# An encoder block on one core: the output projection by seven block products, the memory halves split early, the mixer's residual by accumulating DMAs, the last stores on ScalarE's queue

## The chip, the cores and the metric

The kernel runs on one core of a Trainium2 chip. The metric is the device time of one execution in microseconds (us). Beside the times of plain runs there is one profiled execution, whose trace holds every instruction of the engines and every DMA. The engines are PE (TensorE, with PEld for its weight loads), DVE (VectorE), ACT (ScalarE), POOL (GpSimd) and SP (SyncE, which here only issues DMAs). A "Q" behind an engine's name stands for its sequencer.

## The reference

One layer of an encoder on `x` (512 tokens x 2048, float32), with three sub-layers on the residual stream:

```
h   = rms_norm(x, g_mix_pre);  proj = h @ w_in
mix = concat(diff_attention(8 heads), stick_breaking(8 heads)) @ w_out   # each head normalised on its own
x   = x + rms_norm(mix, g_mix_post)
h   = rms_norm(x, g_mem_pre);  k, v = split(rms_norm(mem, g_mem_kv) @ w_mkv)   # 256 memory tokens, 4 heads
x   = x + rms_norm(softmax(h @ w_mq @ k^T / sqrt(512)) @ v @ w_mo, g_mem_post)
h   = rms_norm(x, g_ffn_pre);  gu = h @ w_gate_up
x   = x + rms_norm((silu(gu[:5632]) * gu[5632:]) @ w_down, g_ffn_post)
```

All inputs and the output are float32.

## The kernel before

Matrix products run on PE in the type fp32r. To keep float32 accuracy each operand is split into a high half h (a rounding copy, on ACT) and a low half l (the difference, on DVE), and each product is made of three matmuls, h·h, h·l and l·h. So each pass over a tile of 128x512 results costs three matmuls.

Weights come in chunks of 128x1024 (512 KB). `Weights` holds the list `chunks` in the order of use; a chunk is loaded into one of the `raws` tiles (five, NR; eight, NW, in some stages) on SP's queue (L120), split by ACT (L131) and DVE (L132) into one of three slots of `parts`, and used by PE (L254). A raw tile is free again once its chunk is split. A chunk's split runs up to two chunks ahead of PE.

`w_v` (and the gate, up and down projections) use a seven-product block scheme, class `Blocks`: the 2x2 blocks of activations and weights are combined so that seven block products stand for eight. Sums of weight blocks are formed while loading: `"load"` with two blocks is a plain load and an accumulating DMA (POOL's queue, L122 and L140) into the same raw tile, `"add"` accumulates one more block onto a raw tile that an earlier product used. The sums of the activations' blocks (`in_forms`) and the sums of the seven results (`evict`) are DVE work.

The output projection `w_out` does not use it: 4 column blocks x 4 token tiles x 16 k tiles x 3 matmuls of 128x512 = 768 matmuls, its 40 chunks (the last column block is done in two halves and loaded twice) by plain loads. The mixed heads come from `subnorm`, one 128x512 tile `mixT` per head, split by `split_mix` into `big`. `Sub.evict` multiplies each result by the post gain; `Sub.residual` (L1157) adds the residual `xres`, which `load_x` (L1103) has loaded, and stores the sum to `x2_d` (L1159); `turn` transposes the result on PE (L1166) and splits it into `big`. `Sub.chain` runs these steps for one token tile, in small steps between PE's matmuls (`side`, `side2`).

The memory attention is folded into its weights: `fold_keys` multiplies `w_mq` by the memory keys (two pairs of heads, 16 rows r each, 24 matmuls of 128x256 each), then come scores and softmax, then `fold_values` on `w_mo`. Keys and values of the memory are made at the start and lie in DRAM (`kT_d`, `vT_d`) as float32; `load_keys` and `load_values` load them back (`kraw`, `vraw`) and split them just before use.

At the end, the eight results of token tiles 0 and 1 are finished by `finish_dma` (scaled, the residual added by an accumulating DMA of POOL's queue, L1135, stored by SP, L1136), the eight of tiles 2 and 3 by `finish` (DVE, L1142; stored by SP, L1145).

The order on every engine is set when the program is built: `fill` runs a step of the side generators every so many matmuls, and a scheduler places each instruction on its engine.

## Time and profile before

| | |
|---|---|
| median of 3 runs (lowest, highest) | 2673.8 us (2672.63, 2677.52) |
| the profiled execution: its own time | 2675.06 us |
| the profiled execution: span from first to last instruction | 2673.2 us |
| busy share of the span: PE, DVE, ACT, POOL | 99%, 62%, 50%, 10% |
| mean granted TensorE clock | 0.997 of full speed |
| DMA | 491.14 MB, mean 184 GB/s |

Line numbers (L254) are those of the kernel before. "a<-b" is an instruction that writes tile a from tile b; 128x512 is partitions x elements. In a row of waits the engine on the left waited for the instruction on the right. The lines of the changed kernel have other numbers: L254, L257 and L258 became L262, L265 and L266; L120, L131, L132 and L140 became L128, L139, L140 and L148; L1136 and L1145 became L1186 and L1195; L1166 became L1238.

### The profile page before, as it was taken

Reading aid. Unit: us, or ns where it says so; the run is one execution under the profiler, and the core shown is the slowest. Engines: PE = TensorE matmul, PEld = TensorE weight load, DVE = VectorE, ACT = ScalarE, POOL = GpSimd, SP = SyncE. Lnnn points to the kernel's source line nnn. Section 1 sums busy time; section 2 is a strip of 40 time slices with the busy share of each in tenths; the row PEclk is TensorE's granted clock in tenths of the full one; section 3 lists DMA queues with packets and bytes.
Section 4 is the critical chain, followed back from the end, with each engine's and each line's share of the span. In section 5 each row is a group of like instructions: output and inputs, shape, how many; then the busy total and the mean of one; then the engine's idle time right before and its main releaser. Section 6 shows DMA issues by size and latency. Waiting matters only on the chain.

```text
span 2673.2 us, 33720 instructions
## 1 busy us (share of the span) xinstructions
PE 2638.9 (99%) x12608; PEld 2194.4 (82%) x12608; DVE 1667.2 (62%) x2295; ACT 1341.0 (50%) x1962; POOL 269.0 (10%) x319
## 2 busy tenths in 40 slices
PE   8999999999999999999999999999999999999997
PEld 7888887778888889988888888888888888878775
DVE  6796556775555366543577665555556568786776
ACT  5555434555665355432455444444444456554554
POOL 0001200000000000000001211211111121102112
PEclk9999999999999999999999999999999999999998
DMA  8889932222222374323558999988888998788888
GB/s 291 284 263 263 231 125 95 85 89 87 71 71 75 126 261 165 115 91 115 162 185 197 250 243 221 196 201 205 204 206 197 210 227 244 195 269 213 214 198 209
DMA packets 171077, 491.14 MB, mean 184 GB/s; under 512 B 18976, under 2 KB 29624, under 8 KB 170912
## 3 DMA queue, kind: packets, MB, share of 16 engines
q1 hardware_dynamic: 129376, 346.47, 38.8%
q0 software_dynamic: 41536, 142.51, 29.0%
q8 instruction: 99, 1.62, 0.3%
q14 instruction: 66, 0.54, 0.1%
HBM read 447.99 MB, written 43.54 MB: 184 GB/s over the span
## 4 chain that ended last, share of the span: by engine, by line
PE 89%; issue 6%; DMA 2%; DVE 1%; POOL 1%; ACT 1%; POOLq 0%; DVEq 0%; SPq 0%; ACTq 0%
PE ps L254 87%; DMA raws<-in_w_dn_dram 1%; PE ps L1509 1%; DVE parts L132 1%; POOL y_d L1625 1%; PE ps L1166 1%; DMA xnat<-in_x_dram 0%; ACT parts L131 0%; PE ps L978 0%; POOL raws L140 0%; DMA kT_d<-memev 0%; POOL raw L140 0%; DMA small<-in_gains_dram 0%; PE ps L1302 0%; DVE raws L137 0%
## 5 line engine op out<-in xcount | busy, mean ns | idle before, releaser
L254 PE MATMUL ps<-parts,big 128*128 128x512 f32 x4608 | 1068.5, 390 | 6.1 <-DVE parts L132 2.8
L132 DVE TENSOR_TENSOR parts<-raws,parts 128x1024 fp32r<-128x1024 f32 x551 | 672.8, 1223 | 555.9 <-ACT parts L131 551.7
L254 PEld LDWEIGHTS ps<-parts,big 128*128 128x128 f32 x4608 | 862.6, 188 | 189.3 <-DVE parts L132 7.5
L131 ACT CAST parts<-raws 128x1024 fp32r<-128x1024 f32 x551 | 579.6, 1052 | 697.1 <-PE ps L254 625.8
L254 PE MATMUL ps<-parts,form 128*128 128x512 f32 x2376 | 550.2, 390 | 2.8 <-ACT parts L131 1.6
L254 PEld LDWEIGHTS ps<-parts,form 128*128 128x128 f32 x2376 | 444.5, 188 | 97.7 <-DVE parts L132 3.6
L254 PE MATMUL ps<-big,parts 128*128 128x512 f32 x1536 | 380.5, 395 | 0.0
L254 PEld LDWEIGHTS ps<-big,parts 128*128 128x128 f32 x1536 | 281.8, 188 | 62.2 <-issue 3.7
L132 DVE TENSOR_TENSOR parts<-raw,parts 128x1024 fp32r<-128x1024 f32 x178 | 217.2, 1222 | 154.2 <-ACT parts L131 153.9
L131 ACT CAST parts<-raw 128x1024 fp32r<-128x1024 f32 x178 | 187.5, 1053 | 194.6 <-PE ps L254 151.0
L254 PE MATMUL ps<-memhl,parts 128*128 128x512 f32 (+1 forms) x1024 | 185.1, 343 | 8.8 <-DVE memhl L265 7.2
L254 PEld LDWEIGHTS ps<-memhl,parts 128*128 128x128 f32 x1024 | 158.9, 191 | 33.6 <-DVE memhl L265 7.2
L140 POOL DMA_DIRECT2D raws<-in_w_gu_dram x108 | 93.3, 864 | 827.3 <-DVE parts L132 699.2
L254 PE MATMUL ps<-khl,parts 128*128 128x256 f32 x768 | 96.2, 285 | 0.0
L418 POOL TENSOR_TENSOR small<-small 128x1 f32<-128x1 f32 (+2 forms) x18 | 12.5, 700 | 824.7 <-DVE small L417 805.6
L254 PEld LDWEIGHTS ps<-khl,parts 128*128 128x128 f32 x768 | 93.3, 192 | 0.2
L254 PE MATMUL ps<-big,pTh 128*128 128x512 f32 x256 | 80.1, 392 | 0.0
L254 PE MATMUL ps<-gh,big 128*128 128x512 f32 x256 | 79.2, 389 | 0.0
L955 ACT ACTIVATE e<-e,small 128x512 f32<-128x512 f32 (+3 forms) x64 | 35.5, 555 | 62.1 <-DVE small L953 62.1
L140 POOL DMA_DIRECT2D raw<-in_w_gu_dram x60 | 51.8, 864 | 114.5 <-DVE parts L132 114.5
L254 PE MATMUL ps<-parts,inh 128*128 128x512 f32 x192 | 59.1, 389 | 0.0
L254 PEld LDWEIGHTS ps<-gh,big 128*128 128x128 f32 x256 | 48.1, 188 | 10.0
(791 smaller groups left out, 2361.9 us busy)
## 6 DMA issues: line engine op xcount, KB each, us to landing
raws<-in_w_gu_dram POOLq DMA_DIRECT2D x113, 512.0 KB, 6.4
raws<-in_w_gu_dram SPq DMA_DIRECT2D x80, 512.0 KB, 4.2
raws<-in_w_qk_dram SPq DMA_DIRECT2D x64, 512.0 KB, 3.4
raw<-in_w_gu_dram POOLq DMA_DIRECT2D x63, 512.0 KB, 5.9
raw<-in_w_gu_dram SPq DMA_DIRECT2D x60, 512.0 KB, 4.2
aq<-actT_d SPq DMA_DIRECT2D x90, 256.0 KB, 5.1
raws<-in_w_dn_dram SPq DMA_DIRECT2D x41, 512.0 KB, 4.9
raws<-in_w_out_dram SPq DMA_DIRECT2D x40, 512.0 KB, 3.4
```

The source lines that it names most:

```text
L131: self.nc.scalar.copy(h, r)
L132: self.nc.vector.tensor_tensor(l, r, h.bitcast(F32), op=ALU.subtract)
L140: self.nc.gpsimd.dma_start(r, self.chunks[m][3], accum_op=ALU.add)
L254: nc.tensor.matmul(o, l, r, start=start, stop=stop, skip_group_check=True)
L418: nc.gpsimd.tensor_tensor(dst, t, mhalf[:, 0:n], op=ALU.pow)
L955: nc.scalar.activation(es[m][:, 0:n], es[m][:, 0:n], AF.Exp, bias=nmx[:, m : m + 1], accum_out=z[:, m : m + 1],)
L1166: nc.tensor.transpose(tp[:, k * P : (k + 1) * P], h[:, k * P : (k + 1) * P], ident)
L1509: nc.tensor.transpose(tp[:, k * P : (k + 1) * P], f[:, k * P : (k + 1) * P], ident)
L1625: nc.gpsimd.dma_start(y_d[t, cb], c, accum_op=ALU.add)
```

## The change

1. `w_out` is computed by `Blocks` in seven products for each of two pairs of column blocks: 7 x 2 x (4 chunks x 2 k x 2 token halves x 3) = 672 matmuls. Products 1 and 7, which only need heads 0 to 7, run first for both pairs, between the last heads. 40 plain loads and 32 accumulating loads bring the weights; products 7 and 5 have both in one chunk. `mix_forms` makes the sums of activation blocks on DVE.
2. The residual after `w_out` is an accumulating DMA: `residual_dma` scales the result by r1 and the gain in one DVE instruction, POOL's queue adds `x` from DRAM, and SP stores the sum. `xres` is not loaded there any more.
3. `split_memory` splits keys and values during the heads' stage and stores both halves (`khl_d`, `vhl_d`); `load_keys` and `load_values` load halves and split nothing.
4. The stores of `finish` go to ScalarE's queue.
5. `subnorm` squares on ACT instead of DVE and ends in two instructions of 256 columns.

```diff
+EARLY, ORDER_MIX = (1, 7), (5, 3, 6, 2, 4)
+MAKE_MIX = {1: ("load", (0, 0)), 7: ("load", (1, 1), (0, 1)), 2: ("load", (1, 0)),
+            3: ("load", (1, 1)), 5: ("load", (0, 0), (0, 1)), 6: ("add", 5, (1, 1)),
+            4: ("add", 6, (1, 0))}
+MIX_WAIT = 8.0, 4.0, 22.0, 10.0
...
-    for cb in range(NCB):
-        wm("w_out", cb, range(8))
-    wm("w_out", NCB - 1, range(8))
+    for i in EARLY:
+        for cbs in col_pairs:
+            wf("w_out", cbs, 0, 4, (i,), MAKE_MIX)
+    for cbs in col_pairs:
+        wf("w_out", cbs, 0, 4, ORDER_MIX, MAKE_MIX)
...
+    def split_memory():
+        for src, dst in ((kT_d, khl_d), (vT_d, vhl_d)):
+            for k2 in range(KT // 2):
+                r = u2(F32, "mraw")
+                dma(r, src[2 * k2 : 2 * k2 + 2].rearrange("k p m -> p k m") if src is kT_d
+                    else src[k2])
+                yield 6.0
+                for k in range(2):
+                    o = u2(s="mhl")
+                    split(o[:, 0], o[:, 1], r[:, k])
+                    dma(dst[2 * k2 + k], o.bitcast(F32))
+                    yield 6.0
...
-            dma(self.dst[t * P : (t + 1) * P, cb * 512 : (cb + 1) * 512], y)
+            nc.scalar.dma_start(self.dst[t * P : (t + 1) * P, cb * 512 : (cb + 1) * 512], y)
...
+        def residual_dma(self, t):
+            s1, r1 = st(), st()
+            nc.vector.tensor_reduce(s1, self.ss[t], axis=AX.X, op=ALU.add)
+            pow_rstd(r1, s1, 1)
+            ss2 = st(4)
+            for cb in range(NCB):
+                y = self.y[t, cb]
+                nc.vector.scalar_tensor_tensor(
+                    y, y, r1, self.g[cb], op0=ALU.mult, op1=ALU.mult
+                )
+                nc.gpsimd.dma_start(
+                    y, self.src[t * P : (t + 1) * P, cb * 512 : (cb + 1) * 512], accum_op=ALU.add
+                )
+                yield 1.5
+            yield 8.0
+            for cb in range(NCB):
+                y = self.y[t, cb]
+                nc.scalar.activation(junk, y, AF.Square, accum_out=ss2[:, cb : cb + 1])
+                dma(self.dst[t * P : (t + 1) * P, cb * 512 : (cb + 1) * 512], y)
+            return ss2
...
     def load_keys(pair):
+        for k in range(8 * pair, 8 * pair + 8):
+            khl[k] = u2(s="khl")
+            dma(khl[k].bitcast(F32), khl_d[k])
+            yield 2
...
+    for i in EARLY:
+        for n, g in enumerate(pairs):
+            g.product(i)
+            done_mix.add((i, n))
+    mix_raw = wpool.tile([P, NW - NR, 1024], F32, name="mix_raw")
+    W.more([mix_raw[:, i] for i in range(NW - NR)], pairs[1].T[7, 1], n_mix)
+    for n, g in enumerate(pairs):
+        g.every = 1
+        for cb in g.cbs:
+            sub.load_g(cb)
+        for i in ORDER_MIX:
+            if n and i == 6:
+                side.add(load_keys(0))
+            g.product(i)
...
-    def load_values(c2s, early):
-        for c2 in c2s:
-            vr = u2(F32, "vraw")
-            dma(vr, vT_d[c2])
+    def load_values(cts, early):
+        for ct in cts:
+            if early:
+                vv = u2(s="vhl")
+                vhl[ct] = (vv[:, 0], vv[:, 1])
+            else:
+                vv = big[:, :, ct, 0:M]
+                vhl[ct] = (big[:, 0, ct, 0:M], big[:, 1, ct, 0:M])
+            dma(vv.bitcast(F32), vhl_d[ct])
```

Three places of the program's order show how it moves instructions. The first is SP's queue between the output projection and `fold_keys`, before the change: the stores `x_d` of the mixer's sums wait for DVE, and the first loads of `w_mq` stand behind all eight of tiles 0 and 1.

```order
L1159 DMA x_d<-y_7149 128x512 [waits DMAHW4_49,DVE_49]
L1159 DMA x_d<-y_7383 128x512 [waits DMAHW5_49,DVE_49]
L1159 DMA x_d<-y_7649 128x512 [waits DMAHW6_49,DVE_49]
L1159 DMA x_d<-y_7801 128x512 [waits DMAHW7_49,DVE_49]
L120 DMA raws<-in_w_mq_dram 128x1024 [waits DMAHW0_49,DVE_49]
L120 DMA raws<-in_w_mq_dram 128x1024 [waits DMAHW1_49,DVE_49]
```

The same place now; "DMASW" is a semaphore of POOL's queue, here that of the accumulating load of the same tile. The last row of `w_mq` ahead of the first store is the chunk of r = 4.

```order
L128 DMA raws<-in_w_mq_dram 128x1024 [waits DMAHW4_49,DMASW1_49,DVE_49]
L1231 DMA x_d<-p__932_7068 128x512 [waits DMAHW5_49,DMASW5_49]
L1231 DMA x_d<-p__982_7551 128x512 [waits DMAHW6_49,DMASW6_49]
L1231 DMA x_d<-p__952_7201 128x512 [waits DMAHW7_49,DMASW7_49]
L1231 DMA x_d<-p__1008_7927 128x512 [waits DMAHW0_49,DMASW0_49]
L128 DMA raws<-in_w_mq_dram 128x1024 [waits DMAHW1_49,DVE_49]
L1231 DMA x_d<-p__933_7070 128x512 [waits DMAHW2_49,DMASW1_49]
L128 DMA raws<-in_w_mq_dram 128x1024 [waits DMAHW3_49,DVE_49]
L1231 DMA x_d<-p__983_7553 128x512 [waits DMAHW4_49,DMASW2_49]
L128 DMA raws<-in_w_mq_dram 128x1024 [waits DMAHW5_49,DVE_49]
```

The stores now wait for accumulating DMAs, and the chunks of r = 5, 6 and 7 stand behind the fourth, the fifth and the sixth store. The second place is the start of `fold_values`: on ACT before the change, where the value halves are copied behind the last exponentials and one weight chunk,

```order
L1288 ACTIVATE ce_9682,small<-ps_9631,small 128x256 [waits DVE_49,PE_49]
L1288 ACTIVATE ce_9682,small<-ps_9631,small 128x256
L131 CAST parts<-raws 128x1024 [waits DMAHW3_49,PE_49]
L257 CAST big<-vraw_9688 128x256 [waits DMAHW1_49]
L257 CAST big<-vraw_9688 128x256
```

and on SP now, where the halves are loaded, each behind a wait for PE (the scores' last matmul that reads that place of `big`):

```order
L1429 DMA vhl_9666<-vhl_d 128x512 [waits PE_49]
L1429 DMA vhl_9692<-vhl_d 128x512 [waits PE_49]
L128 DMA raws<-in_w_mo_dram 128x1024 [waits DMAHW2_49,DVE_49]
L1429 DMA big<-vhl_d 128x2x256 [waits PE_49]
L1429 DMA big<-vhl_d 128x2x256 [waits DMAHW3_49,PE_49]
```

The copies left ACT and DVE, and 14 loads of 256 KB came to SP's queue. The third place is the end of the program. Before, SP has the last stores of tile 1 (L1136) and then the eight of tiles 2 and 3:

```order
L1136 DMA out_dram<-p__1756_19055 128x512 [waits DMAHW3_49,DMASW1_49]
L1136 DMA out_dram<-p__1770_19341 128x512 [waits DMAHW4_49,DMASW2_49]
L1136 DMA out_dram<-p__1779_19514 128x512 [waits DMAHW5_49,DMASW3_49]
L1145 DMA out_dram<-base_19176 128x512 [waits DMAHW6_49,DVE_49]
L1145 DMA out_dram<-p__1749_18982 128x512 [waits DMAHW7_49,DVE_49]
```

Now ACT has them, behind its last activation:

```order
L1728 ACTIVATE junk,small<-base_19695 128x512 [waits DVE_49,Activation_49]
L1195 DMA out_dram<-base_19351 128x512 [waits DMAHW6_49,DVE_49]
L1195 DMA out_dram<-p__1804_19157 128x512 [waits DMAHW7_49,DVE_49]
L1195 DMA out_dram<-p__1828_19569 128x512 [waits DMAHW0_49,DVE_49]
L1195 DMA out_dram<-y_19862 128x512 [waits DMAHW1_49,DVE_49]
L1195 DMA out_dram<-base_19353 128x512 [waits DMAHW2_49,DVE_49]
```

The semaphores DMAHW0 to DMAHW7 go round over all DMAs of SP and ACT. The eight stores of SP ahead of these use DMAHW6, 7, 0 to 5 in this order, so that the k-th store of ACT waits for the landing of SP's k-th store of L1186, as SP's own did before.

## Rows read from the trace of the kernel before

**Rows 1.** The page, its first and fourth parts: busy time of each engine with its share of the span, and the shares of the chain of work that ended last, by engine.

```profile
PE 2638.9 (99%) x12608; PEld 2194.4 (82%) x12608; DVE 1667.2 (62%) x2295; ACT 1341.0 (50%) x1962; POOL 269.0 (10%) x319
PE 89%; issue 6%; DMA 2%; DVE 1%; POOL 1%; ACT 1%; POOLq 0%; DVEq 0%; SPq 0%; ACTq 0%
```

**Rows 2.** Busy time of each engine by stretch of the span: the bounds in us, the length, then for each engine its busy time and number of instructions, the granted TensorE clock as a share of full speed, the busy share of the 16 DMA engines, GB/s. The stretches are the value projection `w_v`, the 16 heads and the output projection `w_out`.

```profile
187.00:340.00 153.00, 153.00 (x687) 126.89 (x686) 96.46 (x113) 73.38 (x86) 28.45 (x33) 1.00 0.98 249
340.00:823.00 483.00, 483.00 (x2376) 391.03 (x2375) 292.34 (x596) 264.19 (x483) 0.00 (x0) 1.00 0.27 87
823.00:994.00 171.00, 170.93 (x773) 141.65 (x772) 79.13 (x98) 71.24 (x114) 2.21 (x3) 1.00 0.47 155
```

**Rows 3.** All waits of PE in the span: what was waited for, us in total, times, longest.

```profile
PE ps L254 <- DVE memhl L265: 7.2, 1, 7.2
PE ps L254 <- DVE parts L132: 5.0, 11, 0.8
PE ps L254 <- ACT parts L131: 4.0, 6, 1.4
PE ps L254 <- ACT big L257: 1.4, 1, 1.4
```

**Rows 4.** The chain that ended last, in `w_out` (matmuls 128x512) and in `fold_keys` (128x256): start, us, engine, what, number of instructions.

```profile
873.42 105.93 PE ps L254 x466
...
1017.16 11.51 PE ps L254 x96
```

**Rows 5.** Two of the waits of all engines in the stretch of `w_v` from 187 to 340 us (us in total, times, longest); the answer has none of PE's matmuls, only PEld, the weight loads.

```profile
ACT parts L131 <- PE ps L254: 74.2, 49, 3.3
PEld ps L254 <- issue: 0.2, 1, 0.2
```

**Rows 6.** A stretch of 11 us in `w_v` and one of 20 us in the mixer's residual; columns as in rows 2.

```profile
231.00:242.00 11.00, 11.00 (x51) 9.09 (x50) 5.01 (x5) 5.37 (x7) 3.45 (x4) 1.00 1.06 211
...
1000.00:1020.00 20.00, 20.00 (x173) 20.00 (x172) 19.12 (x30) 19.63 (x41) 2.00 (x2) 1.00 0.82 295
```

**Rows 7.** The page's third part (DMA queue: packets, MB, time of their packets as a share of 16 engines' span), and DMA issues: tile and tensor, queue, number, KB each, median us from issue to landing.

```profile
q1 hardware_dynamic: 129376, 346.47, 38.8%
q0 software_dynamic: 41536, 142.51, 29.0%
...
raws<-in_w_v_dram POOLq DMA_DIRECT2D x20, 512.0 KB, 9.4
iraw<-in_w_v_dram SPq DMA_DIRECT2D x9, 512.0 KB, 7.1
raws<-in_w_mq_dram SPq DMA_DIRECT2D x32, 512.0 KB, 3.6
```

**Rows 8.** The accumulating loads of `w_v` by their line: the issue on POOL (ns min/median/max, first and last start) and the time from issue to landing.

```profile
L140 POOL DMA_DIRECT2D raws<-in_w_v_dram x20: 853/862/949, 192.7 to 312.5; - x20
...
DMA to landing us min/median/max: 5.2/9.4/11.4
```

**Rows 9.** Instructions of DVE and ACT by line and form: number, busy us, mean ns of one, idle before.

```profile
L132 DVE TENSOR_TENSOR parts<-raws,parts 128x1024 fp32r<-128x1024 f32 x551 | 672.8, 1223 | 555.9 <-ACT parts L131 551.7 <-DMA vr<-v_d 2.9 <-DMA xres<-in_x_dram 0.8
L258 DVE TENSOR_TENSOR big<-mixT,big 128x512 fp32r<-128x512 f32 x15 | 10.0, 687 | 1.3 <-ACT big L257 1.1
L131 ACT CAST parts<-raws 128x1024 fp32r<-128x1024 f32 x551 | 579.6, 1052 | 697.1 <-PE ps L254 625.8 <-issue 19.7 <-DMA raws<-in_w_dn_dram 18.1
```

**Rows 10.** The start of `fold_values` in order of time: PE, ACT and SP (start, us, what, number; in brackets the idle time before it and what ended that).

```profile
1180.70 2.43 PE L254 MATMUL ps<-parts,vhl 128*128 128x512 f32 x10
1184.56 1.65 PE L254 MATMUL ps<-parts,big 128*128 128x512 f32 x6 [1.44 <-ACT big L257]
...
1184.11 2.25 ACT L257 CAST big<-vraw 128x256 fp32r<-128x256 f32 x7
...
1170.69 3.17 SPq L1317 DMA_DIRECT2D vraw<-vT_d  x7
```

**Rows 11.** SP's stores at the end: the first and the last of line 1136 (each waits for one accumulating load of line 1135), and the last of line 1145.

```profile
2650.00 0.34 SPq L1136 DMA_DIRECT2D out_dram<-p__1743_18921  x1
...
2664.25 0.33 SPq L1136 DMA_DIRECT2D out_dram<-p__1779_19514  x1
...
2668.80 0.61 SPq L1145 DMA_DIRECT2D out_dram<-y  x1
```

**Rows 12.** Time from issue to landing of, in this order, the accumulating loads of line 1135, the stores of line 1136 and those of line 1145, all 256 KB.

```profile
DMA to landing us min/median/max: 3.8/8.6/12.8
...
DMA to landing us min/median/max: 2.5/5.4/6.9
...
DMA to landing us min/median/max: 2.6/3.1/3.3
```

**Rows 13.** DVE's last instruction, whose result the last store of line 1145 carries.

```profile
2663.19 0.74 DVE L1142 SCALAR_TENSOR_TENSOR y<-y,small,big 128x512 f32<-128x512 f32 x1
```

**Rows 14.** The end by stretch; columns as in rows 2.

```profile
2658.00:2662.00 4.00, 0.00 (x0) 0.00 (x0) 4.00 (x8) 0.61 (x2) 0.99 (x1) 0.59 1.09 260
2662.00:2664.30 2.30, 0.00 (x0) 0.00 (x0) 1.93 (x3) 0.00 (x0) 0.00 (x0) 0.50 0.99 370
2664.30:2666.00 1.70, 0.00 (x0) 0.00 (x0) 0.00 (x0) 0.00 (x0) 0.00 (x0) 0.50 0.61 228
2666.00:2671.50 5.50, 0.00 (x0) 0.00 (x0) 0.00 (x0) 0.00 (x0) 0.00 (x0) 0.50 0.98 369
```

More of the change, by code (lines that the diff above doesn't have):

```diff
@@ L1043, in sb_gen, with mix_form, first_forms @@
         o = yield from av(w, v, c0)
[L1044 removed]
+        yield from subnorm(o, h, gsb)
+    mixforms = {}
+    def mix_form(i, k2, src, loose=False):
+        if i in HOMES_MIX and not loose:
+            a_, b_ = HOMES_MIX[i]
+            k = 8 * a_ + 2 * k2
+            h, l = (big[:, x, k : k + 2, b_ * M : (b_ + 1) * M] for x in range(2))
+        else:
+            h, l = u2(s="mixh"), u2(s="mixl")
+        split(h, l, src, pin)
+        mixforms[i, k2] = (h, l)
+    def first_forms():
+        for k2 in range(4):
+            while not mixed.issuperset((2 * k2, 2 * k2 + 1)):
+                yield 0
+            mix_form(1, k2, mix[k2, 0], True)
+            yield 12.0
+    side3.add(split_memory())
     vr = load_v(0)
```

173 lines of the change are left out of this document (89 added, 84 removed).

## The prediction

> **What bounds the kernel now.** The page first: PE is busy 99% of the span and makes 89% of the chain that ended last [rows 1], so a change is worth what it takes from PE's work or adds to PE's waits; DVE at 62%, ACT at 50% and the DMA engines matter only where PE waits for them. All waits of PE add up to 17.6 us, of which one, the 1.4 us for ACT's copies into `big`, lies where this change works [rows 3]. By stages: in the 171 us of `w_out` PE is busy 170.93 us, with DMA at 0.47 and DVE at 79 us; in the heads' 483 us DMA is at 0.27 and DVE at 292 us [rows 2]. What is not PE is the end: from 2658 us on PE has nothing, and the DMA engines are at 0.61 to 1.09 [rows 14].
>
> **The matmuls.** `w_out` goes from 768 to 672 matmuls of 128x512; all other products keep their number. In the chain 466 of them take 105.93 us, 0.227 us each [rows 4]. 96 x 0.227 = 21.8 us less. This holds only while PE is fed, so the next parts ask what comes late.
>
> **Feeding PE with weights.** The same scheme runs in `w_v`: 153 us with PE busy all of them, DMA at 0.98, and no wait of a matmul in the list [rows 2, 5]. There, though, a chunk has a load or an accumulate, never both, and eight raw tiles. Here products 7, 7 and 5 of the first pair are 12 chunks with both, on five tiles. Price of one: the stretch of nearly only accumulates moved 211 GB/s at a DMA share of 1.06, so 512 KB (0.524 MB) takes 2.5 us [rows 6]; stores at the end ran at 369 GB/s [rows 14], so a plain load takes 1.4; together 3.9 us against 12 x 0.227 = 2.72 us of matmuls. By the page's means over both queues (346.47 MB at 38.8%, 142.51 MB at 29.0% of 2673.2 us) it is 1.6 + 2.9 = 4.4 us [rows 7]. But the loads start early: a raw tile is free once its chunk is split, so chunk n is loaded some 2.5 us after PE starts chunk n-7. The first eight chunks (products 1 and 1) take 29 us, since 7 us of the last heads' matmuls lie between them, the next eight 24, then 2.72 each: the last of the twelve, the 20th chunk, is needed at 61.6 us and issued 2.5 us behind the start of the 13th, 42.1: 17 us ahead; the first is issued some 6 us into the stage. It needs 3.6 us for the load [rows 7], 5.2 us for the accumulate [rows 8], 1.05 for ACT and 1.22 for DVE [rows 9], 11 us, and what has piled up: the twelve are issued every 3.5 us and served every 3.9, 11 x 0.4 = 4 us. 15 against 17: no stall, by 2 us. At 4.4 us the pile is 10 us and PE waits 4. With nothing started early the loss is 12 x (3.9 - 2.72) = 14 us. I take **1**, near the better-founded price, and keep 0 to 14.
>
> **DVE in the stage.** From product 7 to product 4 of the first pair DVE has, counted in its order, 27 low halves of weights (1.22 us) and 61 operations of 128x512 (0.69) [rows 9]: 27 x 1.22 + 61 x 0.69 = 75 us in 78.6 us of PE. The densest piece is product 2, with 4 and 13 of them: 13.8 us in 10.9, behind product 6 with 9.0 in about 11. A lag of 2.9 us meets a lead of 3 us (the split runs two chunks, 5.4 us, ahead and takes 2.3). In the residual's stretch DVE was busy 19.12 of 20 us, ACT 19.63, and PE all 20 [rows 6]. I take **1**, from 0 to 4.
>
> **The residual by DMA.** Call T0 the end of product 2 of the second pair, when tiles 0 and 1 are complete; a wait of PE here must come before r = 5 of `fold_keys`, at T0 + 10.9 (product 4) + 4 x 2.88 (24 matmuls at 11.51/96 [rows 4]) = T0 + 22.4. Some 6 us later (an estimate: two evictions and two low halves on DVE, 3.8 us by [rows 9], and 2 us for ACT's squares and POOL's small step) eight accumulating loads of 256 KB go out. In the like burst at the end they landed 3.8 us after issue at first, 12.8 us at last [rows 12], one each (2664.25 - 2650.00)/7 = 2.0 us [rows 11]. So tile 0's four land at T0 + 10, 12, 14, 16. SP stands at the first store from there on, and behind it the weight chunk r = 5: issued at T0 + 17, landed 3.6 us later [rows 7], copied 1.05 us later [rows 9]: T0 + 21.7, in time by 0.7. r = 6 stands behind tile 1's first store, T0 + 18: there T0 + 23.7 against T0 + 23, 0.7 late; r = 7 and later have 2.64 us more each against 2.0. I take **0.5**, from 0 to 4 (each landing 0.5 us slower). DVE keeps one operation per result; the `xres` loads that go had cost PE nothing.
>
> **The memory halves.** Now the values come as 14 direct loads from 20 us before `fold_values` on, one every 0.7 us, behind the scores' matmuls that free their place; the first is needed 2.7 us after the start, so ACT's copies at 1184.11 and the 1.44 us of PE behind them go [rows 10]: **-1.4** (0 if a load takes their place). The early splits are 32 operations of 128x256 on ACT and on DVE, each under the 0.69 us of 128x512 [rows 9], 16 loads and 32 stores of 256 KB over the heads' 483 us, where a quarter of the DMA engines and 60% of DVE are used [rows 2]: **0**; if DVE's queue held up a head there, a wait of PE of 1 to 2 us. `subnorm` loses one operation on DVE and gains one on ACT: 0.
>
> **The end.** The eight stores of tiles 2 and 3 leave SP's queue. Their data are ready by 2663.9 [rows 13], they were issued until 2668.80 behind the store at 2664.25 that waits for the last accumulate [rows 11]. By the queue's order ACT could be done sooner; but its eighth store waits for the landing of SP's eighth, 2664.25 + 2.5 [rows 11, 12] = 2666.75 instead of 2668.80: at most 2.05 us. And the DMA engines are full: from 2658 to 2671.5 they were 1.09 x 4 + 0.99 x 2.3 + 0.61 x 1.7 + 0.98 x 5.5 = 13.1 engine-us busy in 13.5 us [rows 14]. Filling the one hole gives 0.66 us; all of it at the highest share, 1.09, takes 12.0 us, a gain of 1.5. If the four first ACT stores push the last accumulate back by their 4 x 0.7 us, the end comes 0.6 us later. I take **-1**, from -2.05 to +0.6.
> The Trainium skill speaks against more here: its page "DMA: Bandwidth & Descriptors", section "Rules for kernel authors", says that spreading DMAs over SP, ACT and GpSimd doesn't raise bandwidth, since all run on the same 16 engines, and saves issue time alone. By that rule the term is the hole, -0.7, and by the queue's order it would be -2.05; the shares near 1 agree with the rule.
>
> **Sum.** -21.8 + 1 + 1 + 0.5 - 1.4 + 0 - 1 = -21.7. The profiled execution took 2675.06 us by its own time (span 2673.2), which gives 2653.4; it stood 1.3 us above the median of the runs, 2673.8. So **2652 us**.
>
> **The rivals.** *Weights late* (the pile in products 7, 7 and 5 decides): +13 us, about 2665. For it: 3.9 us against 2.72, five tiles, and `w_v`'s accumulates took 9.4 us in the median under load [rows 8]. Against it: the 20 us of lead. *DVE the bound in products 2 and 4*: each of the two pairs adds its 2.9 us and as much again for results that hold up others, +6: 2658. For it 75 in 78.6 us; against it [rows 6]. *SP's queue*: accumulates at their slowest landing, +4: 2656. *Slower*: the five raw tiles set the pace. If each chunk with both DMAs holds its tile for 7.1 us of load [rows 7], 0.9 of POOL's issue, 11.4 of accumulate [rows 8] and 2.3 of split, 21.7 us, five tiles give one chunk per 4.3 us; 16 such chunks (products 7, 7, 5, 5) lose 16 x 1.6 = 26 us, and the 16 of products 6 and 4 (0.9 + 11.4 + 2.3 = 14.6, per fifth 2.9) 3 us more. Without any lead the sum is -24.2 of gains, +29, +1 for DVE, +0.5 for the queue: 6 us slower, 2680. It ends slower from 3.6 us per chunk on. Against it: those landings come from eight tiles in flight that queue behind each other; with five the queue is shorter. That the change doesn't do what it says is no rival for the matmuls, whose number the program fixes; for the end it is (gain 0, 2653).
>
> **How the numbers follow.** The likeliest, 0.66: 2652, with a range of its own of 2648 to 2659 (all gains at their best and no stall: 2673.8 - 21.8 - 1.4 - 2 = 2648.6; stalls of 4, 3 and 2 us and no gain at the end: 2659). Weights late 0.12, DVE 0.08, SP's queue 0.05, slower 0.04; 0.05 for what I don't see, in the heads or in `fold_keys`, half of it slower. Range 2647 to 2665. 0.2%, 5.3 us, is about what a measurement can tell from no change. Faster 0.91, same 0.03, slower 0.06.
>
> **What would show it.** The `w_out` stage at about 153 us without waits of PE; no wait for `big` at `fold_values`; ACT's last store some 2 us behind SP's last, and a DMA share near 1 from 2650 us on without the hole. Wrong: waits of PE for `parts` in products 7 and 5 (weights), for DVE's `parts` in product 2 or 4 (DVE), for ACT's `parts` behind an SP wait for accumulating DMAs at r = 5 or 6 (queue).

## The result and the profile after

The changed kernel takes 2678.1 us in the median of its runs (2675.4 to 2683.4) against 2672.7 us before in the same measurement: 1.0019 times as long, with a 95% interval of 1.0012 to 1.0025. It is 5.4 us slower, where 22 us less were forecast. The profiled execution took 2677.1 us by its own time (span 2675.3).

The page of the changed kernel, first and fourth parts, as [rows 1]:

```profile
PE 2627.7 (98%) x12512; PEld 2176.5 (81%) x12512; DVE 1699.1 (64%) x2357; ACT 1381.0 (52%) x2022; POOL 309.8 (12%) x367
...
PE 83%; issue 5%; DMA 5%; DVE 3%; POOL 1%; ACT 1%; SPq 0%; DVEq 0%; POOLq 0%; ACTq 0%
```

PE has its 96 instructions less (12512 for 12608), yet is busy only 11.2 us less, and more of the chain that ended last runs through DMA (5% for 2%) and DVE (3% for 1%). The stretches of [rows 2] and the second of [rows 6], columns as there (the work in them is not quite the same, since the changed kernel reaches `fold_keys` some 9 us sooner):

```profile
187.00:340.00 153.00, 151.97 (x679) 125.18 (x678) 94.94 (x113) 73.29 (x86) 28.46 (x33) 1.00 0.97 248
340.00:823.00 483.00, 480.92 (x2354) 388.62 (x2353) 288.03 (x619) 277.96 (x518) 0.86 (x1) 1.00 0.34 113
823.00:994.00 171.00, 166.24 (x759) 134.71 (x758) 126.63 (x168) 106.63 (x162) 38.74 (x46) 0.99 0.95 244
1000.00:1020.00 20.00, 16.05 (x123) 16.05 (x124) 10.47 (x17) 12.79 (x25) 1.10 (x2) 0.83 1.08 311
```

PE was busy all the time in these before (170.93 of 171 us in `w_out`) and stands in each of them now: 1.0, 2.1, 4.8 and 4.0 us. In the last one it also ran part of the time at its lower clock (granted 0.83 on the mean) and did 123 matmuls instead of 173. DMA went from 0.47 to 0.95 in `w_out` and from 0.82 to 1.08 in the residual. PE's largest waits, as [rows 3] (us in total, times, longest):

```profile
PE ps L262 <- DVE parts L140: 9.8, 18, 1.2
PE ps L262 <- ACT parts L139: 9.1, 8, 4.2
```

`parts`, the split weights, cost 18.9 us of waits for 9.0 before. A wait of 2.1 us for `sqh` (the squares of a head's normalisation) is new; its row stands below.

**In `w_out`.** SP's loads of the twelve chunks that have an accumulating load as well and of one more, the first of product 3, in one row of SP's queue (start, us from the first to the last). Then the time from issue to landing, as far as it is recorded, of the twelve plain loads, of their twelve accumulating loads, and of the three `mix_raw` loads issued at 873.3 to 874.3 us:

```profile
818.23 46.54 SPq L128 DMA_DIRECT2D raws<-in_w_out_dram  x13
...
DMA to landing us min/median/max: 3.3/7.0/9.5
...
DMA to landing us min/median/max: 7.1/8.1/11.2
...
DMA to landing us min/median/max: 8.6/12.0/15.3
```

One load each (46.54 - 0.33)/12 = 3.85 us, where PE uses a chunk in 2.72. The chain that ended last shows why (start, us, what); the last row is DVE's own:

```profile
830.80 5.46 DMA raws<-in_w_out_dram
...
836.80 9.53 DMA raws<-in_w_out_dram
...
847.48 1.24 DVE parts L140
...
848.73 7.23 DMA raws<-in_w_out_dram
...
856.50 9.30 DMA raws<-in_w_out_dram
...
866.96 1.23 DVE L140 TENSOR_TENSOR parts<-raws,parts 128x1024 fp32r<-128x1024 f32 x1 [2.54 <-ACT parts L139]
```

This is one raw tile: load, accumulate, copy, low half, and only then the load of the next chunk into the same tile. The first round is 848.73 - 830.80 = 17.9 us, the second 866.96 + 1.23 - 848.73 = 19.5 us. Read one by one in the same way, the twelve chunks take 16.7 to 20.4 us from the issue of the load to the end of the low half. The mean, 18.9 us, over five tiles is 3.8 us per chunk, close to the 3.85 us of SP's row.

**In the residual.** The low halves of chunks r = 0 and 1 on DVE, which set their tiles free for r = 5 and 6, SP's queue (start, us), the time from issue to landing of the weight loads issued between 989 and 996 us (recorded for r = 6 and 7 alone), ACT's copy of r = 5, and PE (in brackets the idle time before, and what ended it):

```profile
984.69 2.36 DVE L140 TENSOR_TENSOR parts<-raws,parts 128x1024 fp32r<-128x1024 f32 x2
...
983.17 0.33 SPq L1231 DMA_DIRECT2D x_d<-p__932_7068  x1
...
988.89 0.39 SPq L1231 DMA_DIRECT2D x_d<-p__1008_7927  x1
989.37 1.58 SPq L128 DMA_DIRECT2D raws<-in_w_mq_dram  x1
...
DMA to landing us min/median/max: 10.3/11.1/11.9
...
997.70 1.04 ACT L139 CAST parts<-raws 128x1024 fp32r<-128x1024 f32 x1 [3.18 <-DMA raws<-in_w_mq_dram]
...
998.80 0.51 PE L262 MATMUL ps<-khl,parts 128*128 128x256 f32 x2 [1.30 <-ACT parts L139]
...
1003.95 0.80 PE L262 MATMUL ps<-khl,parts 128*128 128x256 f32 x2 [4.21 <-ACT parts L139]
```

The stores stand on SP where the prediction put them, the chunk r = 5 behind them, and PE waits for it and the next. Eight accumulating loads, those of tiles 0 and 1, went out from 979.3 to 985.3 us, and eight more from 992.3 us; these are the bursts meant below. The tiles of r = 5 and 6 were free at 985.9 and 987.0 us, so the stores held these loads up by 3.5 and 5.4 us (r = 6 was issued at 992.5). What differs from the prediction is the landing: r = 5 took 997.70 - 989.37 = 8.3 us to ACT's copy, which waited for it, r = 6 and 7 took 10.3 and 11.9 us, instead of 3.6 [rows 7].

**At the end of `w_v`.** The first load of `split_memory`, issued at 313.21 us (issue to landing), and what stood for it on ACT and on DVE:

```profile
DMA to landing us min/median/max: 13.6/13.6/13.6
...
326.85 0.41 ACT L265 CAST mhl<-mraw 128x256 fp32r<-128x256 f32 x1 [5.64 <-DMA mraw<-kT_d]
...
327.29 0.42 DVE L266 TENSOR_TENSOR mhl<-mraw,mhl 128x256 fp32r<-128x256 f32 x1 [4.82 <-ACT mhl L265]
```

PE's two waits for `parts` behind it add up to the 1.0 us that are missing in `w_v` above.

**Between heads 7 and 8.** PE, and a stretch just behind its wait (columns as above, the clock third from the end):

```profile
630.71 0.86 PE L262 MATMUL ps<-big,parts 128*128 128x512 f32 x3
633.65 0.50 PE L262 MATMUL ps<-sqh,consts_r 128*128 128x512 f32 x1 [2.08 <-ACT sqh L265]
...
635.20:638.20 3.00, 3.00 (x8) 2.30 (x7) 2.17 (x5) 2.39 (x5) 0.00 (x0) 0.50 0.37 145
```

Only three matmuls stand between head 7's last product and the one that needs its squares. Behind the wait PE runs for 3 us at a granted clock of 0.50, its lower level (1.2 GHz): of the eight matmuls in the row the first runs in from before, and seven start in these 3.00 us, so 3.00 - 7 x 0.227 = 1.4 us more are lost. The 4.2 us in the residual have such a tail too (granted 0.62 on the mean from 1004 to 1008 us).

**`fold_values` and the end.** PE at the start of `fold_values`, as [rows 10]; then the end: PE's last row, the last stores of SP and of ACT, and two stretches behind SP's last store, as [rows 11, 14]:

```profile
1181.17 2.88 PE L262 MATMUL ps<-parts,vhl 128*128 128x512 f32 x12
1183.89 4.25 PE L262 MATMUL ps<-parts,big 128*128 128x512 f32 x18
...
2656.77 2.55 PE L262 MATMUL ps<-parts,form 128*128 128x512 f32 x10 [0.53 <-DVE parts L140]
...
2666.04 0.33 SPq L1186 DMA_DIRECT2D out_dram<-p__1834_19689  x1
...
2670.84 0.34 ACTq L1195 DMA_DIRECT2D out_dram<-y  x1
...
2666.00:2668.00 2.00, 0.00 (x0) 0.00 (x0) 0.66 (x1) 0.00 (x0) 0.00 (x0) 0.50 1.05 406
2668.00:2670.00 2.00, 0.00 (x0) 0.00 (x0) 0.00 (x0) 0.00 (x0) 0.00 (x0) 0.50 1.06 408
```

The wait for `big` at `fold_values` is gone. The span ends 16.0 us behind PE's last row.

### The profile page after: what moved, and what is told of

The parts are those of the page before. It is cut to its first block, busy times and chain, and to the rows that moved or that the text cites. A ratio compares the mean times of both kernels' runs of the same rounds, so it can differ in the third digit from the quotient of the medians.

```text
span 2675.3 us, 33895 instructions
## 1 busy us (share of the span) xinstructions
PE 2627.7 (98%) x12512; PEld 2176.5 (81%) x12512; DVE 1699.1 (64%) x2357; ACT 1381.0 (52%) x2022; POOL 309.8 (12%) x367
## 4 chain that ended last, share of the span: by engine, by line
PE 83%; issue 5%; DMA 5%; DVE 3%; POOL 1%; ACT 1%; SPq 0%; DVEq 0%; POOLq 0%; ACTq 0%
PE ps L262 82%; DVE parts L140 1%; DMA raws<-in_w_out_dram 1%; DMA raw<-in_w_dn_dram 1%; DMA raws<-in_w_dn_dram 1%; PE ps L1610 1%; ACT parts L139 1%; DMA mix_raw<-in_w_out_dram 1%; DMA xnat<-in_x_dram 1%; POOL y_d L1726 1%; PE ps L1238 1%; DMA mraw<-kT_d 1%; DMA raws<-in_w_mq_dram 0%; PE ps L1010 0%; POOL raws L148 0%
## 5 line engine op out<-in xcount | busy, mean ns | idle before, releaser
L262 PE MATMUL ps<-parts,big 128*128 128x512 f32 x4368 | 1015.8, 391 | 10.1 <-DVE parts L140 5.4
L262 PEld LDWEIGHTS ps<-parts,big 128*128 128x128 f32 x4368 | 817.8, 188 | 189.9 <-DVE parts L140 12.3
L130 POOL DMA_DIRECT2D raws<-in_w_out_dram x13 | 11.2, 862 | 545.1 <-DMA raws<-in_w_out_dram 545.1
L148 POOL DMA_DIRECT2D raws<-in_w_dn_dram x30 | 26.3, 876 | 266.3 <-DVE parts L140 202.0
```

Of the source, the lines that this page charges most:

```text
L130: self.nc.gpsimd.dma_start(t[0], x, accum_op=ALU.add)
L148: self.nc.gpsimd.dma_start(r, self.chunks[m][3], accum_op=ALU.add)
L262: nc.tensor.matmul(o, l, r, start=start, stop=stop, skip_group_check=True)
```

## The experiments

Differences are between medians; each run's ratio is against the kernel before, whose median was 2672.8 to 2673.3 us in all of them.

### Undoing one part each

**no_memory_split**: `split_memory` and the two halves in DRAM go, `load_keys` and `load_values` are those of before.

```diff
-    side3.add(split_memory())
...
+            kr = u2(F32, "kraw")
+            dma(kr, kT_d[8 * pair + 2 * k2 : 8 * pair + 2 * k2 + 2].rearrange("k p m -> p k m"))
```

> The changed kernel with part 3 undone: keys and values are loaded as float32 and split just before use, as in the kernel before; the rest stays. Theory: of the 5.4 us by which the changed kernel is slower, some 6 us come from the early splits (1.9 us at the end of w_v, where ACT and DVE stand at the split of the first memory tile whose load took 13.6 us; 2.5 us of gap and 1.6 us at half clock near 631 us, between heads 7 and 8), against 1.4 us won at the start of fold_values. Then the time falls by 4 to 5 us against the changed kernel, to 2673 to 2674, the value projection ends as in the kernel before and PE does not wait at 631 us. Rival (the wait at 631 us is the work of the changed subnorm or of the scheduler's order, not of the splits): only the 1.9 us come back and 1.4 us are lost, 2677 to 2678, and PE still waits 2 us for ACT between heads 7 and 8.

Measured: 2674.5 us, 1.0003 (0.9994 to 1.0012): 3.7 us less than the changed kernel. Its stretches of `w_v` and of the heads:

```profile
187.00:340.00 153.00, 153.00 (x686) 126.97 (x685) 95.73 (x113) 74.26 (x86) 28.47 (x33) 1.00 0.97 247
340.00:823.00 483.00, 483.00 (x2378) 391.24 (x2377) 281.26 (x592) 273.62 (x496) 1.73 (x2) 1.00 0.27 89
```

PE is busy all the time in both again, with the changed `subnorm` in place, so both waits belong to the splits, not to `subnorm`. (By the runs alone the difference is at the edge: the two intervals just touch.) In their place stands the old wait of 1.44 us at `fold_values`.

**residual_loaded**: the residual comes by plain loads again.

```diff
-    sub = Sub(GP_MIX, a["x"], x2_d, by_dma=True)
+    sub = Sub(GP_MIX, a["x"], x2_d)
...
+            later.append(lambda: nc.vector.tensor_tensor(c, c, sub.g[cb], op=ALU.mult))
...
+            if n and i == 4:
+                for t in range(NT):
+                    sub.load_x(t)
```

> The changed kernel with part 2 undone: the residual x comes by plain loads into xres and is added by DVE; the post gain is multiplied in by one more DVE instruction for each of the 16 results. Theory: the 16 accumulating loads between 979 and 1018 us keep the weights of fold_keys from landing (8 to 12 us from issue to landing) and cost PE 6.1 us of gaps and 3.5 us at half clock; without them the time falls by 8 to 10 us, to 2668 to 2670, PE busy in all of 950 to 1050 us. Rival (DVE and ACT are late there, not the DMAs): the added DVE work makes it worse, 2678 or more.

Measured: 2669.2 us, 0.9985 (0.9976 to 0.9994): 8.9 us less than the changed kernel, in spite of 16 more instructions on DVE. From 940 to 1050 us PE was busy 108.0 us (changed 104.3), not all 110: two waits of about 1 us for weights stay near 1008 us.

**residual_stores_act**: the stores of the residual's sum on ACT's queue.

```diff
                 nc.scalar.activation(junk, y, AF.Square, accum_out=ss2[:, cb : cb + 1])
-                dma(self.dst[t * P : (t + 1) * P, cb * 512 : (cb + 1) * 512], y)
+                nc.scalar.dma_start(self.dst[t * P : (t + 1) * P, cb * 512 : (cb + 1) * 512], y)
```

> The changed kernel with one change: the 16 stores of the residual sum to x2_d are issued by ACT's queue instead of SP's, so that the weight loads of fold_keys do not stand behind stores that wait for accumulating loads. If the order of SP's queue is what delays the weights: r = 5 is issued some 8 us earlier, before the accumulates of tiles 2 and 3, PE's waits at 997 and 999 us go, and the time falls by 8 to 10 us to about 2669. If the DMA engines' bandwidth is what delays them (8 to 12 us from issue to landing whatever the order), the time falls by less than 3 us, to 2675 to 2678, and PE still waits for ACT's copies there.

Measured: 2681.6 us, 1.0033 (1.0020 to 1.0045), 3.4 us more. By the expectation this speaks for bandwidth and against the order of SP's queue; the trace shows that the run does not separate the two. The low halves of chunks r = 0 and 1 on DVE, the time to landing of the weight loads issued between 988 and 994 us, ACT ahead of its copy of r = 5, and PE:

```profile
987.07 2.36 DVE L140 TENSOR_TENSOR parts<-raws,parts 128x1024 fp32r<-128x1024 f32 x2
...
DMA to landing us min/median/max: 10.7/11.1/11.4
...
997.26 0.63 ACT L1331 ACTIVATE junk<-r__1019_8007 128x512 f32<-128x512 f32 x1 [2.75 <-DMA p__983_7553<-in_x_dram]
...
999.55 0.50 PE L262 MATMUL ps<-khl,parts 128*128 128x256 f32 x2 [2.34 <-ACT parts L139]
...
1004.45 0.80 PE L262 MATMUL ps<-khl,parts 128*128 128x256 f32 x2 [2.09 <-ACT parts L139]
```

With no store in front of it, r = 5 was issued at 988.3 us, as soon as its tile was free, when DVE had the low half of chunk r = 0 (987.07 + 1.2). The whole stage runs 2.4 us later here than in the changed kernel (987.07 against 984.69), so that is 3.4 us sooner than there. Eight accumulating loads were out by then, and the next loads still took some 11 us. PE still waits, some 6 us in three pieces. But ACT, which now issues the stores, stood for accumulating loads ahead of its copy of r = 5 (2.75 us before 997.26), so a part of this wait can come from the new place of the stores. How much of the changed kernel's wait is SP's order and how much the slow landing is therefore not shown. The row on DVE points to a third possibility, the one that keys_8_tiles tests: there are five tiles, and the first load that reuses one comes into the burst. The burst of tiles 2 and 3 began at 1000.3 us instead of 992.3, and PE had waits for weights until 1033 us; that the 3.4 us more come from there is likely, but no run shows it.

**no_accumulate_7_5**: no second weight block in products 7 and 5.

```diff
-MAKE_MIX = {1: ("load", (0, 0)), 7: ("load", (1, 1), (0, 1)), 2: ("load", (1, 0)),
-            3: ("load", (1, 1)), 5: ("load", (0, 0), (0, 1)), 6: ("add", 5, (1, 1)),
+MAKE_MIX = {1: ("load", (0, 0)), 7: ("load", (1, 1)), 2: ("load", (1, 0)),
+            3: ("load", (1, 1)), 5: ("load", (0, 0)), 6: ("add", 5, (1, 1)),
```

> The changed kernel without the 16 accumulating loads of products 7 and 5 of w_out: the second weight block is left out of these two products, so the output is not the reference's; the number of plain loads, of matmuls and all the rest stay. Theory (the weights' supply on five raw tiles costs 8 us between 860 and 895 us): the DMA share falls to about 0.7 there, the waits of PE for parts in products 7 and 5 go, and the time falls by 7 to 9 us to 2669 to 2671. Rival (the low halves are late because DVE's and ACT's queues hold the last head's normalisation and the forms ahead of them): the loads land sooner but PE still waits for parts at 867 to 872 us, and no more than 4 us are won.

Measured: 2666.8 us, 0.9982 (0.9973 to 0.9991): 11.4 us less, at a DMA share of 0.44 instead of 0.96 from 823 to 850 us and 0.82 instead of 1.04 from 850 to 895. DVE and ACT have the same work to do there and are in time, so it is the weights' supply. The loss is larger than the 8 us read from the gaps.

**end_stores_sp**: the last stores on SP's queue.

```diff
-            nc.scalar.dma_start(self.dst[t * P : (t + 1) * P, cb * 512 : (cb + 1) * 512], y)
+            dma(self.dst[t * P : (t + 1) * P, cb * 512 : (cb + 1) * 512], y)
```

> The changed kernel with part 4 undone: the eight stores of token tiles 2 and 3 are issued by SP as before. The time from PE's last matmul to the end of the span goes back from 16.4 to 17.0 us; the whole is 0.6 to 1 us slower, 2679, less than the runs can tell. Rival (by the order of SP's queue): 2 us slower, 18.4 us behind PE's end.

Measured: 2676.4 us, 1.0012 (1.0003 to 1.0021), 1.8 us less, which its interval and that of the changed kernel don't separate. PE's last row and SP's last store:

```profile
2658.48 2.56 PE L262 MATMUL ps<-parts,form 128*128 128x512 f32 x10 [0.53 <-DVE parts L140]
...
2672.19 0.60 SPq L1195 DMA_DIRECT2D out_dram<-y  x1
```

The span (2677.2 us) ends 16.2 us behind PE, against 16.0 with ACT's queue. The part is worth nothing that can be measured.

### Five tiles or eight

**product_and_end**: residual_loaded and no_memory_split together (both edits above).

> Parts 2 and 3 undone together: what stays of the change are the seven products, the stores at the end and the changed subnorm. If the losses of the two parts are separate, they add: the changed kernel's 2678.1 less 3.7 (no_memory_split) and less 8.9 (residual_loaded) gives 2665.5, 7 us faster than before. Rival (both parts only moved load away from the same crowded DMA time, so that one's gain is the other's): the gain is that of the larger alone, 2669.

Measured: 2666.9 us (2660.9 to 2670.1), 0.9972 (0.9962 to 0.9983): 11.3 us less than the changed kernel, where the two alone give 12.6. Within the intervals the two losses add up. (The profiled execution, from which the row of product_and_end below is taken, was the fastest of the seven.)

**product_8_tiles**: as product_and_end, and the three further raw tiles from the first chunk of `w_out` on.

```diff
+    mix_raw = wpool.tile([P, NW - NR, 1024], F32, name="mix_raw")
+    W.more([mix_raw[:, i] for i in range(NW - NR)], mix[0, 0][:, 0], n_mix)
     side3.add(mix_forms())
...
-    mix_raw = wpool.tile([P, NW - NR, 1024], F32, name="mix_raw")
-    W.more([mix_raw[:, i] for i in range(NW - NR)], pairs[1].T[7, 1], n_mix)
```

> As product_and_end, and w_out has its three further raw tiles from the first chunk on instead of from the end of product 7. If it is the number of tiles that paces the weights (each tile is bound for 20 us and more by a load, an accumulate and a split): three chunks more are in flight, PE's waits for parts in products 7 and 5 go, and the time falls by 6 to 9 us against product_and_end, to 2657 to 2660. If it is the DMA engines (share 0.95 to 1.01 in 850 to 950 us), the three tiles only give some 8 us of lead and the queues grow longer: 0 to 3 us less, 2663 to 2665, and PE still waits for parts.

Measured: 2656.1 us (2655.1 to 2658.2), 0.9936 (0.9922 to 0.9950): 10.7 us less by these lines alone. The stretch of products 5 and 3 with five tiles (product_and_end):

```profile
870.00:895.00 25.00, 21.73 (x88) 15.53 (x87) 19.24 (x24) 17.02 (x24) 3.45 (x4) 1.00 0.99 259
```

and with eight (product_8_tiles):

```profile
870.00:895.00 25.00, 24.79 (x108) 19.66 (x107) 20.34 (x25) 17.87 (x26) 3.45 (x4) 1.00 0.82 189
```

The eight tiles take away no byte. Three chunks are loaded ahead, before the last heads are done, and the chain of load, accumulate and split through one tile no longer sets the pace.

**product_no_accumulate**: as product_and_end, with the edit of no_accumulate_7_5.

> As product_and_end, and without the 16 accumulating loads of products 7 and 5 (their second weight block is left out, so the output is not the reference's). This is the sum of the prediction without the three losses: 2672.8 before, less 21.8 for the matmuls and 1 for the end, plus a stall of 1 to 2 us, gives 2651 to 2653, and the stage from 823 to 994 us has PE busy all the time. If a loss is left that the comparison of the traces has not shown, the time is 2656 or more.

Measured: 2659.0 us, 0.9951 (0.9938 to 0.9963), 6 to 8 us over the sum, so by the expectation a loss is left. PE was busy 169.7 of 171 us in the stretch from 823 to 994. Waits for weights stand near 958 and 998 to 1000 us, 2.6 us together; the 1.4 us at `fold_values` are those of the kernel before. The rest is not explained by a row.

**out_8_tiles**: the changed kernel with the edit of product_8_tiles.

> The changed kernel with all its parts, where w_out has its three further raw tiles from the first chunk on instead of from the end of product 7. product_8_tiles won 10.7 us over product_and_end by this alone. If the five tiles set the pace in the changed kernel too, the waits for parts between 860 and 895 us go and the time falls by 8 to 11 us, to 2667 to 2670; the residual's waits near 1000 us stay at 6 us. Rival (the three tiles help only where the rest of the DMA load is gone): less than 4 us, 2674 or more.

Measured: 2667.0 us, 0.9979 (0.9970 to 0.9988): 11.2 us less. From 850 to 870 us the DMA share was 1.03 (changed 1.05) and PE busy all 20 us (changed 19.5). The waits near 990 us stayed. The accumulating loads of products 7 and 5 issued between 815 and 880 us took as long to land as with five tiles (7.1/8.1/11.2 above):

```profile
DMA to landing us min/median/max: 7.2/8.1/10.1
```

**keys_8_tiles**: the changed kernel, whose three tiles are kept for 16 chunks of `w_mq`.

```diff
-    W.more([mix_raw[:, i] for i in range(NW - NR)], pairs[1].T[7, 1], n_mix)
+    W.more([mix_raw[:, i] for i in range(NW - NR)], pairs[1].T[7, 1], n_mix + 16)
```

> The changed kernel with all its parts, where the three further raw tiles are kept through the first 16 chunks of w_mq instead of being given up at the end of w_out. Theory A (lead): the weights of fold_keys are late because with five tiles chunk r = 5 can only be issued when chunk r = 0 has been split, in the middle of the 16 accumulating loads; with eight, r = 5 to 7 are loaded before them and PE's 6 us of waits near 1000 us go with the half clock behind them: 8 to 10 us less, 2668 to 2670. Theory B (bandwidth): the 16 accumulating loads, 16 stores and the weights need more of the DMA engines than the stretch has (share 0.89 in 940 to 1050 us), so the wait only moves three chunks back: less than 4 us won, 2674 or more, and PE waits for parts between 1005 and 1030 us instead.

Measured: 2668.9 us, 0.9980 (0.9971 to 0.9989): 9.3 us less. The stretch of the residual in the changed kernel:

```profile
940.00:1050.00 110.00, 104.29 (x653) 94.60 (x652) 77.81 (x106) 66.48 (x112) 24.10 (x28) 0.97 0.89 260
```

and here, with the time to landing of the loads into `raws` issued between 989 and 1000 us:

```profile
940.00:1050.00 110.00, 109.68 (x688) 98.81 (x687) 80.26 (x110) 67.97 (x117) 24.99 (x28) 1.00 0.89 260
...
DMA to landing us min/median/max: 9.2/14.5/19.1
```

The same DMA share, the same GB/s, the same 16 accumulating loads, and weights that take 14.5 us in the median to land, longer than in the changed kernel: and PE waits 0.3 us, because the three chunks in front of them were issued at 973.9, 977.1 and 980.7 us, two before the burst and one at its start. That is theory A; bandwidth (B) has fallen. These three also stand in front of the stores on SP, so the lead covers both the slow landing and the 3.5 and 5.4 us behind the stores; the run does not tell one from the other.

**all_8_tiles**: both edits, the tiles from the first chunk of `w_out` through 16 chunks of `w_mq`.

> The changed kernel with all its parts and the three further raw tiles from the first chunk of w_out through the first 16 of w_mq. If tiles are what both stages lacked, the two gains add: 2678.1 less 8 to 11 and less 8 to 10, 2658 to 2662; what is left of the losses is then that of the early splits, some 4 us. If the residual is a matter of bandwidth, it comes out as out_8_tiles, 2667 to 2670.

Measured: 2659.8 us, 0.9949 (0.9936 to 0.9961): 18.3 us less than the changed kernel with every one of its parts in place. PE is busy 170.55 of 171 us from 823 to 994 and 109.69 of 110 from 940 to 1050.

### The splits and the best version

**splits_later**: as all_8_tiles, the splits begun behind the first head.

```diff
-    side3.add(split_memory())
...
+            if h == 0:
+                side3.add(split_memory())
```

The order of PE at head 7 that the program fixes, on the left in the kernel before, all_8_no_split and values_split, on the right in the changed kernel, all_8_tiles and splits_later (`ps<-big,parts` is the next projection, `sqh` the squares):

```
ps<-big,parts 128x512 x18          ps<-big,parts 128x512 x3
ps<-sqh,... 128x512                ps<-sqh,... 128x512
```

> As all_8_tiles, with the early splits begun behind the first head instead of at the end of w_v. In its order of PE the normalisation's first matmul of head 7 still stands 3 matmuls behind that head's last product (18 in the kernel before). If the first load's 13.6 us and the order at head 7 are two separate causes: PE's waits at 327 to 333 us go and the 2.5 us near 631 us stay, 1.5 to 2 us less than all_8_tiles, 2658. If DVE or ACT simply have too much to do in the heads' stage, the wait near 631 us moves or goes with the splits' new place.

Measured: 2659.5 us (2656.0 to 2663.6), 0.9950 (0.9938 to 0.9963), by the runs no different from all_8_tiles. The trace tells the two waits apart, `w_v` and then PE at head 7:

```profile
187.00:340.00 153.00, 153.00 (x687) 127.00 (x687) 96.19 (x113) 73.95 (x86) 28.47 (x33) 1.00 0.97 249
...
631.77 0.50 PE L262 MATMUL ps<-sqh,consts_r 128*128 128x512 f32 x1 [2.08 <-ACT sqh L265]
```

The wait in `w_v` went with the late load, the 2.08 us stayed with the order. They are two causes.

**all_8_no_split**: as all_8_tiles, with the edit of no_memory_split.

> As all_8_tiles, without the early splits (keys and values are split just before use, as before). In its order of PE 18 matmuls stand again between head 7's last product and the normalisation's matmul. Expected: both waits go (5.5 us) and the 1.4 us at fold_values with its half clock comes back, 2655 to 2656, as product_8_tiles (2656.1), which differs from it by the residual alone. If the residual by accumulating loads still costs something with eight tiles, the time is 2658 or more.

Measured: 2655.7 us, 0.9938 (0.9925 to 0.9952), as expected: 4.1 us less than all_8_tiles (by medians of five runs each, whose intervals overlap), and with eight tiles the residual by accumulating loads is not measurably dearer than by plain loads (product_8_tiles, 2656.1).

**values_split**: as product_8_tiles, the tiles kept for 16 chunks of `w_mq`, and only the values split early, behind the first head.

```diff
+            if h == 0:
+                side3.add(split_values())
```

> As product_8_tiles (residual by plain loads, keys split just before use), with the three tiles kept through the first 16 chunks of w_mq, and only the values split early, starting behind the first head instead of at the end of w_v. Expected against product_8_tiles (2656.1): the 2.1 us of wait near 997 us and the 1.8 us at the start of fold_values go, 2652 to 2653. Rival (the early splits disturb the order of the heads wherever they lie, as near 631 us): 2656 or more, with a wait of PE for ACT between two heads.

Measured: 2654.0 us (2650.9 to 2656.4), 0.9927 (0.9915 to 0.9940): the lowest median of all, 19 us less than the kernel before and 24 less than the changed one; its interval overlaps with those of all_8_no_split and product_8_tiles. PE's busy time, from the page, and all of PE's waits:

```profile
PE 2618.7 (99%) x12512; PEld 2175.8 (82%) x12512; DVE 1707.3 (64%) x2389; ACT 1381.8 (52%) x2022; POOL 298.0 (11%) x351
...
PE ps L262 <- DVE memhl L273: 6.9, 1, 6.9
PE ps L262 <- DVE parts L140: 5.8, 13, 0.9
PE ps L262 <- ACT parts L139: 5.7, 6, 1.2
```

## Why the prediction was wrong

**The matmuls** (-21.8) were right in their number, 96 instructions less, and near in their price: in values_split, where little waits, PE is busy 20.2 us less than before (2618.7 for 2638.9 us). Its time is 19 us below the kernel before, where the matmuls, the 1.4 us at `fold_values` and the 0.6 us at the end would give 24. all_8_no_split lacks as much (17.4 for 22.4). No row explains these 5 us.

**Weights** (1 taken, 0 to 14): 11.2 us by out_8_tiles, near the far end. The rival *weights late* (+13 us, at 0.12) names the place and nearly the size. The working had the right objects, a lead of 17 us against a need of 15, and decided by 2 us between numbers that were not known so closely. The step that failed is the need, with its 3.6 us for the load and 5.2 us for the accumulate: 3.6 is the median of another stage, and 5.2 is the fastest of the twenty in [rows 8], whose median is 9.4. Here the loads landed in 3.3 to 9.5 us and the accumulates in 7.1 to 11.2, and a chunk took 16.7 to 20.4 us from the issue of its load to the end of its split, instead of 15. The sum slips as well: from 6 to 42.1 us in eleven steps the twelve are issued every 3.3 us, not every 3.5, so the pile is 7 us, the need 18, and the margin is gone on paper already. In the trace the issue came out the other way: every 3.85 us, since each load waits for a tile. Product 3's plain loads, behind product 6's accumulating ones, landed in 8.6 to 15.3 us. The rival *slower* had the mechanism and nearly its numbers (21.7 us for a tile, 4.3 us per chunk; measured 18.9 and 3.8; its "slower from 3.6 us per chunk on" does not follow from its own terms, which give 3.9). It was set aside with the sentence that with five tiles in flight the queue is shorter: the accumulating loads landed in 7.1 to 11.2 us, median 8.1, with five tiles and in 7.2 to 10.1, median 8.1, with eight (out_8_tiles). Its time, 2680, came near the measured 2678 by another sum, which is luck: the lead held for the first chunks, so the tiles cost less in `w_out` than its 29 us, and the rest came from places that it did not have.

**The residual** (0.5 taken, 0 to 4): 9.3 us by keys_8_tiles, outside the bounds. The accumulating loads of the first tile landed at 983 to 989 us, 8 to 14 us behind the end of product 2, where 10 to 16 were worked out, SP stood for them as said, and r = 5 was issued 14.5 us behind that end, sooner than the 17 worked out. The step that failed is "landed 3.6 us later [rows 7]": that is the median of all 32 loads of `w_mq`, and this one comes behind eight accumulating loads and beside eight more. It took 8.3 us, and the next two 10.3 and 11.9. The rival *SP's queue* is neither shown nor refuted: the stores held r = 5 and 6 up by 3.5 and 5.4 us, and residual_stores_act, which took them off SP, made ACT wait for them. It was priced by slower accumulates, which is not what came. keys_8_tiles shows that three chunks more of lead cover both; that r = 5 reuses the tile of chunk 0, so that five tiles put it into the burst, the working had not weighed.

**The splits** (0 taken, 1 to 2 if DVE held up a head): 5.5 us, the 4.1 of all_8_no_split (3.7 by no_memory_split) and the 1.4 that they win at `fold_values`. The step that failed is the 0, taken from the mean load of a stage. The mean of the stage (a quarter of the DMA engines) hid that the first load is issued in the stage before, at a share of 0.97; and ACT and DVE, which take their instructions in order, stood 5.6 and 4.8 us for it. At head 7 the splits changed what the scheduler puts between a product and its normalisation; the order of the changed kernel shows it, and it wasn't looked at there.

**`fold_values`** (-1.4) was right, and **DVE in the stage** (1) leaves at most 0.5 us with eight tiles (all_8_tiles, PE busy 170.55 of 171 us). **The end** (-1): 16.0 us behind PE's last row instead of 16.6, -0.6, which by end_stores_sp is not due to the queue: 16.2 there. ACT's last store followed SP's last by 4.8 us, not by the 2.5 worked out, with the DMA engines at 1.05 and 1.06 between; the hole of [rows 14] was not there. The Trainium skill says in "DMA: Bandwidth & Descriptors", section "Rules for kernel authors", that spreading DMAs over the queues doesn't raise bandwidth and saves issue time alone. This trace agrees: the engines were full, and the time stayed.

Sum with what the runs showed: -21.8 + 11.2 + 9.3 + 5.5 - 1.4 - 0.6 = +2.2. The medians differ by 5.4; the 3 us between stay open, and the intervals of the three measured terms (some 2 to 4 us either way for each) leave room for them. That the spans of the two profiled executions differ by 2.1 is luck: the seven-product stages behind, which the change does not touch, took 1214.6 us in the one before and 1218.0 in the changed kernel, from the first to the last matmul on a `form` tile. In the other runs they took 1214.2 to 1221.2 us, and no row explains what makes them differ.

## What to carry to other kernels

A load's price is the one of the stretch in which it is issued, behind what is issued there; a median over a stage, or a busy share over one, says nothing of the first load and of the load behind a burst. Where weights go through a few tiles, work out how long one tile is bound (load, accumulate, split, and what stands in front of the split) and divide by their number; if that is above what PE needs per chunk, count the lead in chunks, and give the stage its further tiles before the dense piece, not behind it. A sum that turns on a margin of 2 us in 17 should add up the landings of a loaded stretch, not the fastest one on record, and give the far end (here *weights late*, 0.12) far more.

## What the runs showed of the hardware

- At the same DMA share (0.89) and the same GB/s (260), from 940 to 1050 us, PE stood 5.7 us in one kernel and 0.3 in the other: a high DMA share is no sign of a loss by itself. Three chunks of 512 KB loaded ahead made the difference.
- An accumulating load of 512 KB took 7.1 to 11.2 us from issue to landing with five tiles and 7.2 to 10.1 with eight, 8.1 in the median of both, at DMA shares of 1.05 and 1.03 from 850 to 870 us. Fewer tiles in flight did not make them land sooner here.
- After one gap of PE, the 2.08 us that ended at 633.65 us, the granted clock was 0.50 from 635.2 to 638.2, which adds 1.4 us to the wait.
